# A segment mean on one core: looks 15 rows ahead, probe copies 9 rows ahead of them, and a start in two groups of three rows

## The chip, the core and the metric

The kernel runs on one core of a Trainium2 chip. TensorE (PE), VectorE (DVE), ScalarE (ACT), GpSimd (POOL) and SyncE (SP) each work through their own instructions in order and wait for each other on semaphores; 16 DMA engines move data between HBM and the on-chip memory. The metric is the device time of one execution in microseconds.

## What is computed

Ten million numbers come with sorted segment ids between 0 and 9999; the result is the mean of each segment.

```python
sums = np.zeros(num_segments); counts = np.zeros(num_segments)
np.add.at(sums, segment_ids, data)
np.add.at(counts, segment_ids, 1)
return sums / np.maximum(counts, 1)
```

## The kernel before

The numbers lie as 128 partitions of 78125, and each partition is worked off in 90 rows of 875. The ids are sorted and a segment has about a thousand numbers, so most rows hold one border between two segments, and the kernel reads only the ids around it. For a row it needs:

- probes: every 175th id of the row. One copy brings those of a whole group of rows into `pr` (`load_probes`, L161), 30 columns of 8 bytes per partition for six rows.
- the look (`first_look`, L259): six small VectorE instructions per group (`SG` L274, `ST`, `far`, `ST`, `IDX` L290, `YY` L293) that find from the probes between which two of them the border lies. `gather` (L305) then has GpSimd fetch per row and partition a window of 175 ids from there, 179 kB, into one of 18 slots of `GT`.
- the sum of that window on ScalarE (`add_ids`, L317, into `GS`); it runs up to six rows ahead of the row that ScalarE is at.
- the second look (L330) on VectorE: the border's place `KK` for a group of rows from `YY` and `GS`.
- the row itself: ScalarE sums all of it (`total`, L343), VectorE the part in front of the border (`split`, L348). Data come in tiles of two rows (875 kB) in 18 buffers, issued by SP.

Between rows VectorE also works out counts, running sums and places (steps hung up in the table `after` with `put(row, steps)`), and the last instructions make the output.

Everything is written out in one order by hand (manual schedule): the loop at L855 goes through the rows, and each engine gets its instructions in the order of that loop. Probe copies of the first `HEAD` groups are issued by SP, the others by GpSimd (L164), `X_POOL` = 18 rows ahead of their group; looks are at `X_LOOK` = 9 rows ahead. As GpSimd issues gathers and copies in order, they stand in one queue: six gathers, a copy, six gathers, a copy. A gather's slot must have been summed 18 rows earlier.

Of the kernel before, what the change touches and what calls it, by code (L numbers as in the profile page):

```python
# [17 lines left out]
P = 128  # L18
# [4 lines left out]
NR = 90  # L23
# [3 lines left out]
E = 20  # L27
NX = NR + E
FAR = float(1 << 18)
GROUPS = [6] * 15  # L30
X_PROBE = 11
X_POOL = 18
X_DATA = 26
X_LOOK = 9
RING = 18
IDS = 87
HALVES = 66
# [2 lines left out]
ND = 2 * SHIFT + 1  # L40
NT1 = 91
M1 = 8
R1 = 8 * M1 - 2
R2 = NR + 4
RM = 78
# [74 lines left out]
def kernel(  # L120
# [24 lines left out]
    def x_sum(r):  # L145
        return 6 if r < HALVES else 4
# [6 lines left out]
    snt32 = snt.bitcast(I32)  # L153
# [3 lines left out]
    bounds = [0]  # L157
# [3 lines left out]
    def load_probes(g):  # L161
        a = 0 if g == 0 else K * bounds[g] + 1
        b = min(K * bounds[g + 1] + 1, NPR)
        e = nc.sync if g < HEAD else nc.gpsimd  # L164
        e.dma_start(out=pr_flat[:, a:b], in_=ids_p[:, a * S : (b - 1) * S + 1 : S])  # L165

    tiles = {}

    def load_data(t):
        d = dpool.tile([P, 2 * L], FP32, name="data_t")  # L170
        a, b = 2 * t * L, min(2 * (t + 1) * L, D)
        c = b if t < NT - 1 else a + L
# [13 lines left out]
    def view(ap, dims):  # L186
# [3 lines left out]
        out=gt32[:, :, 0 : 2 * W : 2], in_=view(q5[:, 0, 0:1], [[0, RING], [0, W]]), func=ACT.Copy  # L190
# [30 lines left out]
        out=plast, in0=pc, scalar1=float(P - 1), scalar2=1.0e6, op0=ALU.is_equal, op1=ALU.mult  # L221
# [5 lines left out]
        out=sp_i, in0=sp_i, scalar1=3, scalar2=None, op0=ALU.arith_shift_right  # L227
    )
    nc.vector.tensor_copy(out=sp, in_=sp_i)
    ident = cpool.tile([P, P + 1], FP32, name="ident")  # L230
    nc.vector.memset(ident, 0.0)
    make_identity(nc, ident[:, 0:P])
    ones = cpool.tile([P, P], FP32, name="ones")
    nc.vector.memset(ones, 1.0)
    jj_i = cpool.tile([P, P], I32, name="jj_i")
    jj = cpool.tile([P, P], FP32, name="jj")
    nc.gpsimd.iota(jj_i, pattern=[[1, P]], base=0, channel_multiplier=0)  # L237
    nc.vector.tensor_copy(out=jj, in_=jj_i)  # L238


    VI = pr32[:, :, 0]
# [7 lines left out]
    NBP = cpool.tile([P, NX + 1], FP32, name="NBP")  # L249
    NB = NBP[:, 1:]  # L250
    QQ = cpool.tile([P, NX], FP32, name="QQ")
    FFP = cpool.tile([P, NX + 1], FP32, name="FFP")
    FF = FFP[:, 1:]
    nc.vector.memset(NBP, 0.0)
    nc.vector.memset(FFP[:, 0:1], 0.0)
    junk_v = cpool.tile([P, L], BF16, name="junk_v")
    junk_a = cpool.tile([P, L], BF16, name="junk_a")

    def first_look(g):  # L259

        a, b = bounds[g], bounds[g + 1]
        n = b - a
        far = fpool.tile([P, n], FP32, name="far", bufs=3)
        last = b == NR
        v = nc.vector

        def s1():
            if last:
                m = NR * K + 1 - NPR
                v.tensor_copy(  # L270
                    out=pr_flat.bitcast(I32)[:, 2 * NPR : 2 * (NPR + m)].rearrange("p (a b) -> p a b", b=2),
                    in_=view(snt32[:, 0:1], [[0, m], [1, 2]]),
                )
            v.tensor_reduce(out=SG[:, a:b], in_=pr32[:, a:b, 0 : 2 * K : 2], axis=AX.X, op=ALU.add)  # L274

        def s2():
            v.scalar_tensor_tensor(  # L277
                out=ST[:, a:b], in0=VI[:, a + 1 : b + 1], scalar=float(K), in1=SG[:, a:b],
                op0=ALU.mult, op1=ALU.subtract,
            )  # L280

        def s3():
            v.tensor_scalar(out=far, in0=ST[:, a:b], scalar1=0.0, scalar2=FAR, op0=ALU.is_equal, op1=ALU.mult)  # L283

        def s4():
            v.tensor_add(out=ST[:, a:b], in0=ST[:, a:b], in1=far)  # L286

        def s5():
            for c, d, w in [(a, b - 1, S), (b - 1, b, TAIL)] if last else [(a, b, S)]:
                v.scalar_tensor_tensor(  # L290
                    out=IDX[:, c:d], in0=ST[:, c:d], scalar=float(w), in1=wb[:, c:d], op0=ALU.mult, op1=ALU.add
                )
            v.scalar_tensor_tensor(  # L293
                out=YY[:, a:b], in0=ST[:, a:b], scalar=float(K + 1), in1=SG[:, a:b], op0=ALU.mult, op1=ALU.add
            )
            if last:
                v.tensor_scalar(
                    out=tl, in0=ST[:, NR - 1 : NR], scalar1=-1.0, scalar2=float(TAIL - S),
                    op0=ALU.add, op1=ALU.mult,
                )  # L300
# [57 lines left out]
    KEY = cpool.tile([P, NX + PAD], FP32, name="KEY")  # L358
    RB = cpool.tile([P, R2], FP32, name="RB")
    RX = cpool.tile([P, E], FP32, name="RX")  # L360
    PS = cpool.tile([P, R2 + 1], FP32, name="PS")
    PX = cpool.tile([P, E + 1], FP32, name="PX")
    MX = cpool.tile([P, E], FP32, name="MX")
    XX = cpool.tile([P, NX], FP32, name="XX")
    RF = cpool.tile([P, NX + PAD], FP32, name="RF")
    sel = cpool.tile([P, NT1 // 7, 7, 8], FP32, name="sel")
    tab = cpool.tile([P, NT1], FP32, name="tab")
# [10 lines left out]
    wp = cpool.tile([P, NO - C2], FP32, name="wp")  # L378
    most = cpool.tile([P, NO - C2], FP32, name="most")
    OUT = cpool.tile([P, NO], FP32, name="OUT")  # L380
    nc.vector.memset(RF, 0.0)
    nc.gpsimd.memset(tab, 0.0)
    nc.gpsimd.memset(tax, 0.0)
    nc.gpsimd.memset(shf[:, :, ND : ND + 1], 0.0)
    nc.gpsimd.memset(add, 0.0)
    nc.gpsimd.memset(xa, 0.0)
    nc.vector.memset(PS[:, 0:1], 0.0)
    nc.vector.memset(PX[:, 0:1], 0.0)
    nc.gpsimd.memset(KEY, -1000.0)
    bad = cpool.tile([P, 2 * NX + 8 + NR - RE], FP32, name="bad")  # L390
    j1 = cpool.tile([P, NX], FP32, name="j1")
    j2 = cpool.tile([P, NX], FP32, name="j2")
# [169 lines left out]
    def counts(a, b):  # L562


        n = b - a
        ps = fpool.tile([P, n], FP32, name="ps")
        ct = fpool.tile([P, n], FP32, name="ct")

        def s1():
            nc.vector.tensor_add(out=ps, in0=KK[:, a:b], in1=QQ[:, a:b])  # L570

        def s2():
            nc.vector.tensor_tensor_scan(
                out=PS[:, a + 1 : b + 1], data0=ps, data1=ps, initial=PS[:, a : a + 1],
                op0=ALU.max, op1=ALU.max,
            )
# [12 lines left out]

        return [s1, s2, s3, s4, s5]  # L590
# [183 lines left out]
            general_path(tc, fpool, ppool, data, segment_ids, out2d, jj)  # L774


    NG = len(GROUPS)
    NT = (NR + 1) // 2
    nc.vector.memset(snt32[:, 0:1], NSEG)
    nc.vector.memset(snt32[:, 1:2], 0)  # L780
    HEAD = 3


    after = defaultdict(list)
# [1 line left out]
    def put(r, steps, every=1):  # L786
        for i, f in enumerate(steps):
            after[r + i // every].append(f)

    for g in range(HEAD):  # L790
        after[-1] += first_look(g)
    after[-1] += second_look(0, GROUPS[0])
    for a, b in zip(bounds[1:], bounds[2:]):
        if b == NR:
# [6 lines left out]
            put(a + 2, second_look(a + 3, b))  # L801
    for g in range(HEAD, NG):
        if g < NG - 1:
            put(max(bounds[g] - X_LOOK, 0), first_look(g), 5)

    def mixed(p, q):
        out = []
        for i in range(max(len(p), len(q))):
            out += p[i : i + 1] + q[i : i + 1]
        return out  # L810
# [21 lines left out]
    put(64, place(0, T1, tab, [(0, C1, ND + 1, OUT[:, 0:C1]), (C1, T1, ND + 1, xa[:, 0 : T1 - C1, RM - R1])]))  # L832
    put(70, mixed(keys(72, RE)[1:], pick(nc.vector, pa[:, :, 0 : RM - R1], C1, CA - C1, R1, RM)), 2)
    put(73, check())
    look = bounds[NG - 1] - X_LOOK
    put(70, pick(nc.gpsimd, pb[:, :, 0 : RE - RM], C2, NO - C2, RM, RE), 2)
    put(look, mixed(first_look(NG - 1), counts(R1, RM)), 99)
    put(look, pick(nc.gpsimd, pb[:, :, RE - RM :], C2, NO - C2, RE, R2), 99)
    put(look + 1, mixed(edges_of(RE, NR), []), 99)
    put(look + 2, single(RE, NR, bad[:, 2 * NX + 8 :]) + verdict()[:1], 99)  # L840
# [8 lines left out]
        + spread(RS, R2, pb[:, :, RS - RM :], add[:, :, RS - RM : nb], NO - C2) + total_of(add, most), 99)  # L849
    assert max(after) <= NR - 1  # L850

    pnext = 0
    nt = 0
    gs = 0
    for r in range(-X_PROBE - X_DATA, NR):  # L855
        while pnext < NG and bounds[pnext] <= r + (X_PROBE + X_DATA if pnext < HEAD else X_POOL):
            load_probes(pnext)
            pnext += 1
            if pnext == 1:
                load_data(0)  # L860
                nt = 1
        while nt < NT and 2 * nt <= r + X_DATA:
            load_data(nt)
            nt += 1
        if r == -X_DATA:
            nc.scalar.dma_start(
                out=snt[0 : P - 1, :],
                in_=segment_ids[D : N].rearrange("(p d) -> p d", d=D)[:, 0:1],
            )
        if r == -1:  # L870
            for f in after[r][: 5 * HEAD]:
                f()
        while r >= -1 and gs < IDS and gs <= r + x_sum(gs):
            add_ids(gs)
            gs += 1
        if r == -1:
            for f in after[r][5 * HEAD :]:
                f()
        if r >= 0:
            total(r)  # L880
            split(r)
            for f in after[r]:
                f()
# [31 lines left out]
```

## Time and profile before

| | us |
|---|---|
| median of three runs | 202.51 (202.50 to 202.52) |
| the profiled execution, whole | 202.07 |
| its span, from the first instruction to the last | 200.3 |
| VectorE busy | 142.3 (71%) |
| ScalarE busy | 135.2 (67%) |
| GpSimd busy | 120.4 (60%) |
| first and last `split` (L348) start | 22.41 and 195.55 |

The busy time of GpSimd is the issuing of its copies and gathers; when they land is another matter and is read from who waits for them. TensorE has six matmuls and plays no part.

### The profile page before, as it was taken

Reading aid. Unit: us, or ns where it says so; the run is one execution under the profiler, and the core shown is the slowest. Engines: PE = TensorE matmul, PEld = TensorE weight load, DVE = VectorE, ACT = ScalarE, POOL = GpSimd, SP = SyncE. Lnnn points to the kernel's source line nnn. Section 1 sums busy time; section 2 is a strip of 40 time slices with the busy share of each in tenths; the row PEclk is TensorE's granted clock in tenths of the full one; section 3 lists DMA queues with packets and bytes.
Section 4 is the critical chain, followed back from the end, with each engine's and each line's share of the span. In section 5 each row is a group of like instructions: output and inputs, shape, how many; then the busy total and the mean of one; then the engine's idle time right before and its main releaser. Section 6 shows DMA issues by size and latency. Waiting matters only on the chain.

```text
span 200.3 us, 1426 instructions
## 1 busy us (share of the span) xinstructions
PE 1.6 (1%) x6; PEld 1.4 (1%) x6; DVE 142.3 (71%) x441; ACT 135.2 (67%) x356; POOL 120.4 (60%) x131
## 2 busy tenths in 40 slices
PE   0000000000000100000000000000000000010000
PEld 0000000000000100000000000000000000010000
DVE  6330587159628588493967989469399999999992
ACT  8011599920884949779494983949999499999700
POOL 5677778027875874747668177683746867677000
DMA  5999999999999999999999999999999995250000
GB/s 27 166 248 397 409 405 399 271 201 412 404 253 378 341 291 404 235 405 257 370 354 278 409 240 405 329 294 402 229 405 265 376 291 149 59 116 22 2 0 8
DMA packets 25363, 54.61 MB, mean 273 GB/s; under 512 B 14640, under 2 KB 15784, under 8 KB 25351
## 3 DMA queue, kind: packets, MB, share of 16 engines
q1 hardware_dynamic: 18459, 40.13, 63.4%
q0 software_dynamic: 6720, 14.38, 24.8%
q14 instruction: 12, 0.10, 0.1%
q10 hardware_dynamic: 172, 0.00, 0.1%
HBM read 56.59 MB, written 0.04 MB: 283 GB/s over the span
## 4 chain that ended last, share of the span: by engine, by line
DVE 31%; DMA 30%; issue 19%; ACT 11%; POOL 6%; POOLq 0%; ACTq 0%; DVEq 0%
DMA GT<-in_segment_ids_dram,IDX 25%; DVE junk_v L348 18%; ACT junk_a L343 7%; DMA pr<-in_segment_ids_dram 6%; ACT junk_a L317 4%; POOL GT L307 4%; DVE q L330 1%; POOL pr L165 1%; DVE far L283 1%; DVE ST L277 0%; DVE ST L286 0%; DVE IDX L290 0%; DVE shf L683 0%; DVE SG L274 0%; DVE FFP L601 0%
## 5 line engine op out<-in xcount | busy, mean ns | idle before, releaser
L307 POOL DMA_INDIRECT GT<-in_segment_ids_dram,IDX x90 | 91.3, 1015 | 61.0 <-issue 30.7
L348 DVE SCALAR_TENSOR_TENSOR junk_v<-iota,q,data_t 128x875 bf16<-128x875 f32 x90 | 100.5, 1117 | 1.4
L343 ACT ACTIVATE junk_a<-data_t 128x875 bf16<-128x875 f32 x90 | 83.6, 929 | 2.8
L317 ACT ACTIVATE junk_a<-GT 128x175 bf16<-128x175 int32 x87 | 31.3, 360 | 50.3 <-DMA GT<-in_segment_ids_dram,IDX 39.8
L330 DVE SCALAR_TENSOR_TENSOR q<-YY,GS 128x6 f32<-128x6 f32 (+1 forms) x19 | 3.6, 190 | 34.9 <-ACT junk_a L317 27.3
L165 POOL DMA_DIRECT2D pr<-in_segment_ids_dram x12 | 20.0, 1668 | 0.0
L343 ACT ACTIVATION_READ_ACCUMULATOR junk_a<-data_t 128x1 f32 x90 | 16.8, 186 | 0.0
L317 ACT ACTIVATION_READ_ACCUMULATOR junk_a<-GT 128x1 f32 x87 | 16.2, 186 | 0.0
L274 DVE TENSOR_REDUCE SG<-pr 128x6 f32<-128x30 int32 x15 | 2.7, 181 | 11.8 <-DMA pr<-in_segment_ids_dram 11.7
L348 DVE DVE_READ_ACCUMULATOR junk_v<-iota,q,data_t 128x1 f32 x90 | 7.4, 83 | 0.0
L283 DVE TENSOR_SCALAR far<-ST 128x6 f32<-128x6 f32 x15 | 3.1, 209 | 0.5
L189 ACT ACTIVATE GT<-q 128x3150 int32<-128x3150 f32 x1 | 3.0, 2992 | 0.0
L277 DVE SCALAR_TENSOR_TENSOR ST<-pr,SG 128x6 f32<-128x6 int32 x15 | 2.5, 166 | 0.5
L290 DVE SCALAR_TENSOR_TENSOR IDX<-ST,wb 128x6 int32<-128x6 f32 (+2 forms) x16 | 2.5, 161 | 0.5
L286 DVE TENSOR_TENSOR ST<-ST,far 128x6 f32<-128x6 f32 x15 | 2.5, 165 | 0.5
L293 DVE SCALAR_TENSOR_TENSOR YY<-ST,SG 128x6 f32<-128x6 f32 x15 | 2.4, 162 | 0.0
L189 ACT ACT_TABLE_LOAD x1 | 1.3, 1283 | 0.7 <-PEq L899 0.7
L715 POOL TENSOR_SCALAR pb<-pb 128x168 f32<-128x168 f32 (+1 forms) x2 | 1.6, 785 | 0.2
L555 PE MATMUL badp<-bads,ones 128*128 128x1 f32 x2 | 0.6, 362 | 108.4 <-DVE bads L554 108.4
L601 DVE TENSOR_TENSOR_SCAN FFP<-NBP,FFP,XX 128x8 f32<-128x8 f32 (+3 forms) x5 | 1.3, 265 | 0.1
L238 DVE CAST jj<-jj_i 128x128 f32<-128x128 int32 x1 | 0.8, 839 | 0.7 <-POOL jj_i L237 0.7
L668 DVE TENSOR_TENSOR sel<-sel,RF 128x280 f32<-128x280 f32 (+1 forms) x3 | 1.2, 410 | 0.1
(129 smaller groups left out, 47.4 us busy)
## 6 DMA issues: line engine op xcount, KB each, us to landing
data_t<-in_data_dram SPq DMA_DIRECT2D x44, 875.0 KB
GT<-in_segment_ids_dram,IDX POOLq DMA_INDIRECT x90
data_t<-in_data_dram SPq DMA_DIRECT2D x1, 437.5 KB
pr<-in_segment_ids_dram POOLq DMA_DIRECT2D x11, 30.0 KB
data_t<-in_data_dram SPq DMA_DIRECT2D x1, 125.0 KB
pr<-in_segment_ids_dram SPq DMA_DIRECT2D x2, 30.0 KB
out_dram<-OUT SPq DMA_DIRECT2D x1, 36.6 KB
pr<-in_segment_ids_dram SPq DMA_DIRECT2D x1, 31.0 KB
```

What stands on the lines that cost most here:

```text
L165: e.dma_start(out=pr_flat[:, a:b], in_=ids_p[:, a * S : (b - 1) * S + 1 : S])
L189: nc.scalar.activation(out=gt32[:, :, 0 : 2 * W : 2], in_=view(q5[:, 0, 0:1], [[0, RING], [0, W]]), func=ACT.Copy)
L274: v.tensor_reduce(out=SG[:, a:b], in_=pr32[:, a:b, 0 : 2 * K : 2], axis=AX.X, op=ALU.add)
L277: v.scalar_tensor_tensor(out=ST[:, a:b], in0=VI[:, a + 1 : b + 1], scalar=float(K), in1=SG[:, a:b], op0=ALU.mult, op1=ALU.subtract,)
L283: v.tensor_scalar(out=far, in0=ST[:, a:b], scalar1=0.0, scalar2=FAR, op0=ALU.is_equal, op1=ALU.mult)
L286: v.tensor_add(out=ST[:, a:b], in0=ST[:, a:b], in1=far)
L290: v.scalar_tensor_tensor(out=IDX[:, c:d], in0=ST[:, c:d], scalar=float(w), in1=wb[:, c:d], op0=ALU.mult, op1=ALU.add)
L307: nc.gpsimd.indirect_dma_start(out=GT[:, r % RING, :], out_offset=None, in_=ids2d[:], in_offset=bass.IndirectOffsetOnAxis(ap=IDX[:, r : r ...
L317: nc.scalar.activation(out=junk_a[:, 0:W], in_=gt32[:, r % RING, 0 : 2 * W : 2], func=ACT.Copy, accum_out=GS[:, r : r + 1],)
L330: nc.vector.scalar_tensor_tensor(out=KK[:, a:b], in0=YY[:, a:b], scalar=float(S // K), in1=GS[:, a:b], op0=ALU.mult, op1=ALU.subtract,)
L343: nc.scalar.activation(out=junk_a[:, 0:n], in_=d, func=ACT.Copy, accum_out=t)
L348: nc.vector.scalar_tensor_tensor(out=junk_v[:, 0:n], in0=iota[:, 0:n], scalar=KK[:, r : r + 1], in1=d, op0=ALU.is_lt, op1=ALU.mult, accum_ ...
```

## The change

- Groups: the first six rows become two groups of three, so there are 16 groups; the first four (18 rows) have their looks ahead of row 0 (`HEAD` = 4, before 3).
- Looks are 15 rows ahead instead of 9, all six instructions in one row also for the last group, whose look was at row 75 and is now at row 69.
- Probe copies stand 24 rows ahead of their group. GpSimd issues the first one (16 columns) as its first instruction, SP the next four, between the first data tiles; the sixth is issued by GpSimd between the gathers of the start.
- VectorE's constants that the first look doesn't need move behind that look, GpSimd's fills (`blanks`) behind row 0.

```diff
-GROUPS = [6] * 15
-X_PROBE = 11
-X_POOL = 18
+GROUPS = [3, 3] + [6] * 14
+HEAD = 4
-X_LOOK = 9
+X_LOOK = 15
+X_PROBE = X_LOOK + 9
...
-        e = nc.sync if g < HEAD else nc.gpsimd
+        e = nc.sync if 0 < g <= HEAD else nc.gpsimd
...
+    load_probes(0)
...
-    nc.vector.memset(ident, 0.0)
-    make_identity(nc, ident[:, 0:P])
...
+    def constants():
+
+        nc.vector.tensor_copy(out=jj, in_=jj_i)
+        nc.vector.memset(ident, 0.0)
+        make_identity(nc, ident[:, 0:P])
...
+    def blanks():
+
+        nc.gpsimd.memset(tab, 0.0)
...
-        after[-1] += first_look(g)
+        after[-1] += first_look(g) + ([constants] if g == 0 else [])
...
-            put(max(bounds[g] - X_LOOK, 0), first_look(g), 5)
+            put(bounds[g] - X_LOOK, first_look(g), 5)
...
-    look = bounds[NG - 1] - X_LOOK
+    put(bounds[NG - 1] - X_LOOK, first_look(NG - 1), 5)
+    put(0, [blanks])
+    look = 75
...
-    put(look, mixed(first_look(NG - 1), counts(R1, RM)), 99)
+    put(look, counts(R1, RM), 99)
...
+        if r == -X_DATA:
+            load_probes(1)
+            load_data(0)
+            load_probes(2)
+            load_probes(3)
+            load_data(1)
+            load_probes(4)
+            nt = 2
+        if r >= 0:
+            for g in range(HEAD + 2, NG):
+                if bounds[g] == r + X_PROBE:
+                    load_probes(g)
...
+            for i, f in enumerate(after[r][:looks]):
                 f()
+                if i == 2 * 5:
+                    load_probes(HEAD + 1)
```

GpSimd's instructions from the last fills of the start on, before (`GT` are gathers, `pr` probe copies; the second row stands for rows 0 to 17, the fourth for rows 18 to 23):

```order
L389 MEMSET KEY 128x112
L307 DMA GT<-in_segment_ids_dram,IDX 128x175 x18
L165 DMA pr<-in_segment_ids_dram 128x30x1 x2
L307 DMA GT<-in_segment_ids_dram,IDX 128x175 x6
L165 DMA pr<-in_segment_ids_dram 128x30x1
```

The same with the change, from GpSimd's last iota on (the gathers of rows 0 to 2, 3 to 5, 6 to 17, 18 to 23 and 24 to 29):

```order
L236 IOTA jj_i 128x128
L303 DMA GT<-in_segment_ids_dram,IDX 128x175 x3
masks.py:197 MEMSET ident 128x128
masks.py:199 AFFINE_SELECT ident<-ident 128x128
L303 DMA GT<-in_segment_ids_dram,IDX 128x175 x3
L165 DMA pr<-in_segment_ids_dram 128x30x1
L303 DMA GT<-in_segment_ids_dram,IDX 128x175 x12
L392 MEMSET tab 128x91
...
L397 MEMSET KEY 128x112
L303 DMA GT<-in_segment_ids_dram,IDX 128x175 x6
L165 DMA pr<-in_segment_ids_dram 128x30x1
L303 DMA GT<-in_segment_ids_dram,IDX 128x175 x6
```

One copy instead of two stands ahead of row 18's gather, and the fills have moved from ahead of the first gather to behind the eighteenth. In both, the copy behind the gathers of rows 18 to 23 is the one for rows 30 to 35.

VectorE from row 0 on, before (L330 is a second look, L348 a row, L274 the first instruction of a look, here the one for rows 18 to 23, at row 9):

```order
L330 SCALAR_TENSOR_TENSOR q_74<-YY,GS 128x6
L348 SCALAR_TENSOR_TENSOR junk_v,q_74<-iota,q_74,data_t 128x875 x6
...
L348 SCALAR_TENSOR_TENSOR junk_v,q_74<-iota,q_74,data_t 128x875 x4
L274 TENSOR_REDUCE SG<-pr 128x6
L277 SCALAR_TENSOR_TENSOR ST<-pr,SG 128x6
```

The same with the change (the look for rows 18 to 23 is at row 3):

```order
L326 SCALAR_TENSOR_TENSOR q_75<-YY,GS 128x3
L344 SCALAR_TENSOR_TENSOR junk_v,q_75<-iota,q_75,data_t 128x875 x3
...
L344 SCALAR_TENSOR_TENSOR junk_v,q_75<-iota,q_75,data_t 128x875
L270 TENSOR_REDUCE SG<-pr 128x6
L273 SCALAR_TENSOR_TENSOR ST<-pr,SG 128x6
```

The look has moved up by six rows of L348, and its probe copy with it: SP issues it at the start. From row 15 on, the look at a row is the one that stood six rows later before, and its copy is one that GpSimd issues one group of gathers later than the copy of the look that stood there.

## Rows read from the trace of the kernel before

**Rows 1.** The page, busy time of each engine (share of the span), instructions.

```profile
PE 1.6 (1%) x6; PEld 1.4 (1%) x6; DVE 142.3 (71%) x441; ACT 135.2 (67%) x356; POOL 120.4 (60%) x131
```

**Rows 2.** The page, DMA queues (q1: SP, q0: GpSimd): packets, MB, share.

```profile
q1 hardware_dynamic: 18459, 40.13, 63.4%
q0 software_dynamic: 6720, 14.38, 24.8%
```

**Rows 3.** Waits of all engines: in total us, times, longest us.

```profile
ACT junk_a L317 <- DMA GT<-in_segment_ids_dram,IDX: 39.8, 16, 9.0
...
DVE q L330 <- ACT junk_a L317: 27.3, 9, 5.1
...
DVE SG L274 <- DMA pr<-in_segment_ids_dram: 11.7, 3, 6.2
```

**Rows 4.** Busy time by stretch: PE, PEld, DVE, ACT, POOL, clock, DMA share, GB/s.

```profile
120.00:145.00 25.00, 0.00 (x0) 0.00 (x0) 16.98 (x46) 18.25 (x49) 16.72 (x16) 1.00 1.04 331
145.00:170.00 25.00, 0.00 (x0) 0.00 (x0) 24.46 (x77) 20.78 (x57) 16.87 (x16) 1.00 0.96 301
```

**Rows 5.** VectorE's timeline, 128 to 172 us: start, duration, instruction, [idle before].

```profile
143.38 0.19 DVE L330 SCALAR_TENSOR_TENSOR q<-YY,GS 128x6 f32<-128x6 f32 x1 [3.41 <-ACT junk_a L317]
...
149.45 0.18 DVE L274 TENSOR_REDUCE SG<-pr 128x6 f32<-128x30 int32 x1
...
159.82 0.18 DVE L274 TENSOR_REDUCE SG<-pr 128x6 f32<-128x30 int32 x1
...
161.22 1.12 DVE L348 SCALAR_TENSOR_TENSOR junk_v<-iota,q,data_t 128x875 bf16<-128x875 f32 x1
```

**Rows 6.** ScalarE's timeline, window sums of rows 18, 24 and 72.

```profile
50.39 0.36 ACT L317 ACTIVATE junk_a<-GT 128x175 bf16<-128x175 int32 x1 [9.01 <-DMA GT<-in_segment_ids_dram,IDX]
...
62.66 0.36 ACT L317 ACTIVATE junk_a<-GT 128x175 bf16<-128x175 int32 x1 [3.08 <-DMA GT<-in_segment_ids_dram,IDX]
...
158.56 0.36 ACT L317 ACTIVATE junk_a<-GT 128x175 bf16<-128x175 int32 x1 [2.68 <-DMA GT<-in_segment_ids_dram,IDX]
```

**Rows 7.** GpSimd's timeline: copies, the gathers of rows 18, 24 and 84.

```profile
31.07 3.35 POOL L165 DMA_DIRECT2D pr<-in_segment_ids_dram  x2
43.93 1.09 POOL L307 DMA_INDIRECT GT<-in_segment_ids_dram,IDX  x1 [9.51 <-issue]
...
51.55 1.67 POOL L165 DMA_DIRECT2D pr<-in_segment_ids_dram  x1
53.53 1.04 POOL L307 DMA_INDIRECT GT<-in_segment_ids_dram,IDX  x1 [0.31 <-ACT junk_a L343]
...
172.74 1.11 POOL L307 DMA_INDIRECT GT<-in_segment_ids_dram,IDX  x1 [1.40 <-DVE IDX L290]
```

**Rows 8.** DMA rate, 170 to 182 us, 40 slices of 0.3 us.

```profile
GB/s 61 121 238 107 0 0 0 0 0 0 0 0 0 0 27 154 201 121 14 84 168 201 70 61 131 93 47 164 140 187 168 42 93 177 247 28 15 89 19 0
```

**Rows 9.** DMA rate, 50 to 90 us, 40 slices of 1 us.

```profile
GB/s 394 417 416 375 415 399 410 196 135 139 304 380 407 385 413 393 403 413 338 186 128 167 312 417 370 412 394 423 403 407 332 151 128 181 398 381 406 408 398 413
```

**Rows 10.** ScalarE's timeline, window sum of row 3.

```profile
19.07 0.36 ACT L317 ACTIVATE junk_a<-GT 128x175 bf16<-128x175 int32 x1 [3.70 <-DMA GT<-in_segment_ids_dram,IDX]
```

**Rows 11.** All engines' timeline, the start.

```profile
3.71 0.15 DVE L229 CAST sp<-sp_i 128x1 f32<-128x1 int32 x1
...
4.78 0.17 POOL L382 MEMSET tab<- 128x91 f32 x1
...
5.72 0.18 DVE L274 TENSOR_REDUCE SG<-pr 128x6 f32<-128x30 int32 x1
...
7.72 1.20 POOL L307 DMA_INDIRECT GT<-in_segment_ids_dram,IDX  x1 [1.38 <-DVE YY L293]
...
8.41 30.61 SPq L173 DMA_DIRECT2D data_t<-in_data_dram  x16
```

**Rows 12.** DMA rate, 130 to 170 us, 40 slices of 1 us.

```profile
GB/s 134 164 342 409 381 389 395 400 430 370 345 142 129 164 360 401 399 401 431 420 382 406 267 144 167 247 372 431 382 403 375 383 379 274 82 113 240 127 149 158
```

More of the change, by code (lines that the diff above doesn't have):

```diff
@@ L230 @@
     ident = cpool.tile([P, P + 1], FP32, name="ident")
-    nc.vector.memset(ident, 0.0)
-    make_identity(nc, ident[:, 0:P])
     ones = cpool.tile([P, P], FP32, name="ones")
-    nc.vector.memset(ones, 1.0)
     jj_i = cpool.tile([P, P], I32, name="jj_i")
@@ L237 @@
     nc.gpsimd.iota(jj_i, pattern=[[1, P]], base=0, channel_multiplier=0)
-    nc.vector.tensor_copy(out=jj, in_=jj_i)
     VI = pr32[:, :, 0]
@@ L253 @@
     FF = FFP[:, 1:]
-    nc.vector.memset(NBP, 0.0)
-    nc.vector.memset(FFP[:, 0:1], 0.0)
     junk_v = cpool.tile([P, L], BF16, name="junk_v")
@@ L380 @@
     OUT = cpool.tile([P, NO], FP32, name="OUT")
[L381 to L389, printed above, removed]
+    def constants():
+        nc.vector.tensor_copy(out=jj, in_=jj_i)
+        nc.vector.memset(ident, 0.0)
+        make_identity(nc, ident[:, 0:P])
+        nc.vector.memset(ones, 1.0)
+        nc.vector.memset(RF, 0.0)
+        nc.vector.memset(PS[:, 0:1], 0.0)
+        nc.vector.memset(PX[:, 0:1], 0.0)
+        nc.vector.memset(NBP, 0.0)
+        nc.vector.memset(FFP[:, 0:1], 0.0)
+    def blanks():
+        nc.gpsimd.memset(tab, 0.0)
+        nc.gpsimd.memset(tax, 0.0)
+        nc.gpsimd.memset(shf[:, :, ND : ND + 1], 0.0)
+        nc.gpsimd.memset(add, 0.0)
+        nc.gpsimd.memset(xa, 0.0)
+        nc.gpsimd.memset(KEY, -1000.0)
     bad = cpool.tile([P, 2 * NX + 8 + NR - RE], FP32, name="bad")
@@ L774, in finish @@
             general_path(tc, fpool, ppool, data, segment_ids, out2d, jj)
+    nc.vector.memset(snt32[:, 0:1], NSEG)
+    nc.vector.memset(snt32[:, 1:2], 0)
     NG = len(GROUPS)
     NT = (NR + 1) // 2
-    nc.vector.memset(snt32[:, 0:1], NSEG)
-    nc.vector.memset(snt32[:, 1:2], 0)
-    HEAD = 3
     after = defaultdict(list)
@@ L790 @@
     for g in range(HEAD):
-        after[-1] += first_look(g)
+        after[-1] += first_look(g) + ([constants] if g == 0 else [])
+    looks = len(after[-1])
     after[-1] += second_look(0, GROUPS[0])
@@ L850 @@
     assert max(after) <= NR - 1
-    pnext = 0
     nt = 0
     gs = 0
[L855 to L861, printed above, removed]
+    for r in range(-X_DATA, NR):
+        if r == -X_DATA:
[10 more added lines that the diff above has]
+                    load_probes(g)
         while nt < NT and 2 * nt <= r + X_DATA:
@@ L870 @@
         if r == -1:
-            for f in after[r][: 5 * HEAD]:
+            for i, f in enumerate(after[r][:looks]):
                 f()
+                if i == 2 * 5:
+                    load_probes(HEAD + 1)
         while r >= -1 and gs < IDS and gs <= r + x_sum(gs):
@@ L876 @@
         if r == -1:
-            for f in after[r][5 * HEAD :]:
+            for f in after[r][looks:]:
                 f()
```

## The prediction

> **What bounds the kernel now.** I read the page first. No engine is busy throughout: VectorE leads with 142.3 us, 71% of the span [rows 1], so something makes it wait. The queue lines come next: SP's data copies and GpSimd's id copies together take 88% of the 16 DMA engines' span [rows 2], which leaves the memory side little room. Then the waits over all engines, where the reader is to see one chain: ScalarE waited 39.8 us in 16 pieces for gathers (the window of ids per row, tile `GT`), and VectorE waited 27.3 us in nine pieces for ScalarE's sums of those windows; three looks out of 15 waited for a probe copy, so the other twelve found theirs landed [rows 3]. VectorE never waited for data. The table by stretches puts the waits in their place: from 120 to 145 us VectorE is busy 16.98 of 25, from 145 to 170 it is busy 24.46 of 25, with the DMA share at 1.04 and 0.96 [rows 4]. So there are two stages: until row 60 the gathers set the pace (the last such wait ends at 143.38 [rows 5]); behind it VectorE works without a gap to the end.
>
> What sets the pace of the gathers? ScalarE's wait for the first window of a group ends at 50.39, 62.66 and so on to 158.56, nine groups of six rows later [rows 6]: (158.56 - 50.39) / 9 = 12.02 us per group. GpSimd is not the bound, it had issued early: the gather of row 24 at 53.53, 9.1 us before its ids were added, while the gather of row 18 at 43.93, issued after 9.5 us of idle time with nothing ahead of it, needed 6.5 us [rows 6, 7]. Near the end, with no data moving, the gather issued at 172.74 shows as a burst that ends near 175.5, under 3 us [rows 7, 8]. So beside the data copies the transfers that GpSimd issues stand in line. What they take there: in the rate by 1 us slices a probe copy shows as a dip from 400 to some 130 GB/s, 3.5 to 4 us long (57 to 61, 68 to 72, 80 to 84) [rows 9]; I take 3.7. Then a gather takes (12.02 - 3.7) / 6 = 1.39 us. The dips also show the order: the copy issued at 51.55 moves from 57 on, behind the six gathers issued before it [rows 7, 9].
>
> The Trainium skill, "DMA: Bandwidth & Descriptors", section "Anatomy of one DMA", fits such a transfer at 2.0 us plus its bytes at 436 GB/s, an estimate of 2.4 us for a gather's 179 kB. By that rule no line builds up, and the time would be rival A's. The lone gather at the end agrees with it; the 9.1 us beside data do not, and the measurement decides.
>
> **The change, part by part.**
>
> *Order in the line.* Before, GpSimd sends 18 gathers, two copies (31.07), nothing until 43.93, six gathers, a copy. The gather of row 3 lands at 19.07 [rows 10]. The copy for rows 30 to 35, issued at 51.55, is through at about 61.2 [rows 7, 9]. After, the line behind row 3 is: 2 gathers, one copy, 12 gathers, 6 gathers, and the copy for rows 30 to 35: 20 x 1.39 + 2 x 3.7 = 35.2, so 54.2. The idle stretch and one copy (now SP's) are gone: the line runs 7.0 us earlier, if row 3 lands when it did. From there on it was saturated before and stays so: 12.02 a group.
>
> *The start.* It shifts that 7.0. For: VectorE reaches its first look at 5.72 only because 1.9 us of other constants stand behind the cast at 3.71 [rows 11]; they now come behind the look. Against: GpSimd first issues a copy of 16 columns (30 columns took 1.67 [rows 7], so 1.0 to 1.7), and its iotas, which VectorE's casts wait for, move back by that; about 0.5 us is left. Row 3's window came after a wait of 3.70 us [rows 10], when SP's stream of tiles, issued from 8.41 [rows 11], had set in; SP now sends another copy before its third tile, which puts the stream off by up to 3 us. Bounds for row 5 and the copy behind it: 2.5 us earlier (all of that counts) to 1 us later (GpSimd's first copy lands after VectorE is ready). I take 1.1 earlier, nearer to the middle than to either end. The line is then 8.1 us ahead.
>
> *Looks 15 rows ahead.* This is the term that takes the gain away. VectorE works in order, and a look needs its probe copy. The look at row 63 was for rows 72 to 77; now it is for rows 78 to 83, whose copy stands one group (12.02 us) further back in the line. That copy's dip ends at about 156.5 [rows 12]; minus 8.1 is 148.4. Before, the look at row 63 ran at 149.45 [rows 5], so it starts 1.0 earlier. Without its wait of 3.41 us at row 60 [rows 5] VectorE would be there by about 146, so it stands idle for 2.4. All looks from row 15 on wait like that: queued behind each are VectorE's next rows, whose windows landed before. The look at row 69 needs the last copy, of 26 instead of 30 columns: 12.02 - 0.5 = 11.5 behind the one before, 148.4 + 11.5 = 159.9. VectorE's own work from row 63's look to row 69's, 159.82 - 149.45 = 10.4, would have it there at 158.8, so the copy decides. Before: 159.82. So at row 69 the changed kernel is level, +0.1.
>
> *After row 69* there is one look less: row 75's has moved up. A look took 1.4 at row 69 (159.82 to 161.22 [rows 5]); row 75's ran in the gaps of other work, so between 0.5 and 1.4, I take 1.0. VectorE's remaining work is otherwise the same, and it is the bound there [rows 4].
>
> *Costed at nothing.* VectorE's constants, 1.9 us, stand in its wait for the first windows. GpSimd's fills, which ran from 4.78 on and were over before the gather at 7.72 [rows 11], now stand between the gathers of rows 17 and 18, under 2 us, covered by some 8 us of line; without that they would delay row 18 by themselves. Splitting the first group starts row 0 earlier, but row 15's look waits in any case. SP's extra copy delays its tiles by some 3 us; no wait for data stands among VectorE's waits, so that has cover.
>
> Sum: +0.1 - 1.0 = -0.9 us. The profiled execution took 202.07 us with a span of 200.3; the median of the three runs is 202.51, and against that the forecast is 201.6 us. With the start between its bounds it runs from 200.2 to 203.7.
>
> **Rivals.**
>
> *A: the looks find their copies.* If the line is not served in order or is faster than 1.39 and 3.7 once more is queued, the early looks cost nothing; row 60 moves by the full 8.1 and VectorE saves a look: 202.5 - 9.1 = 193.4; half of it, with 0.6 us less per group, gives about 196. For it: twelve looks did not wait [rows 3]. Against: windows issued six deep still came 12.02 a group. The Trainium skill, same page, section "Queues, rings and completion order", says that a DMA engine takes turns between queues packet by packet. By that rule the line's share beside data does not grow when gathers are issued earlier, which speaks against A and against the change. Chance 0.17.
>
> *B: slower, by the first copy.* Everything in the line hangs on GpSimd's first copy. If it lands near 8 us instead of 5.2 (beside data the copy issued at 51.55 needed 9.7 us [rows 7, 9]), the line is 2.7 us later, 5.4 ahead instead of 8.1, and the look at row 69 starts at 162.6: 201.6 + 2.7 = 204.3. It turns to a loss once the line is less than 7.2 us ahead. Against it: at the start no data stream runs. Chance 0.21.
>
> *C: no change that shows.* What the start gains is small, the looks only trade a wait for gathers for a wait for copies, and the line is 7 to 7.6 us ahead: 202.5. Chance 0.19.
>
> **How the numbers follow.** The forecast has 0.43. A measurement of this kernel can tell 0.2%, 0.4 us, from no change. Faster than 202.1: two thirds of the forecast's own range and all of A, a little of C: 0.47. Slower than 202.9: B, and small parts of the forecast and C: 0.31. The rest, 0.22, is within. The range for 8 in 10 goes from 196.0 (A's half, leaving out A's full gain) to 204.6 (B's price); the forecast's own range, 200.2 to 203.7, lies inside it.
>
> **What would show it.** Right: VectorE's largest wait is the look (`SG`) for probe copies, some ten times 2 to 5 us, and its wait for ScalarE's window sums is nearly gone; windows still come 12 us a group; the look at row 69 starts near 160. The gather of row 18 follows the fills without an idle stretch. Wrong: looks without waits and VectorE full from row 50 on (A); a first gather issued after 9 us (B); groups under 11.5 us apart would break the figure of the line itself.

## The result: slower by 3 us, and the profile after

The changed kernel takes 205.62 us (median, 205.08 to 206.11), the kernel before 202.51: a ratio of 1.015, 95% interval 1.0119 to 1.018. The forecast was 201.6 us and its range ended at 204.6, so the sign and the range were both wrong. The profiled execution took 205.08 us with a span of 203.3; before it was 202.07 and 200.3. Runs more than 1.5% above the fastest of their kernel count in no ratio; below, that concerns two of the four runs with halved data copies on the kernel before.

The page, engine line and SP's and GpSimd's queues, changed kernel:

```profile
PE 1.6 (1%) x6; PEld 1.4 (1%) x6; DVE 142.2 (70%) x448; ACT 135.3 (67%) x356; POOL 120.1 (59%) x131
...
q1 hardware_dynamic: 20267, 40.15, 64.3%
q0 software_dynamic: 6688, 14.36, 22.9%
```

No engine works more than before [rows 1] and the bytes are the same [rows 2]. SP now issues more of the copies in 8-byte pieces, which shows as 1800 more packets. So the loss is in waits. The waits, changed kernel (us in total, times, longest):

```profile
ACT junk_a L313 <- DMA GT<-in_segment_ids_dram,IDX: 45.6, 18, 10.8
DVE SG L270 <- DMA pr<-in_segment_ids_dram: 31.6, 12, 4.5
DVE q L326 <- ACT junk_a L313: 17.9, 4, 9.1
```

Against [rows 3]: looks wait for their probe copies 12 times instead of three, 31.6 us instead of 11.7, and VectorE's wait for window sums has shrunk from 27.3 to 17.9. That is the exchange of one wait for another which was forecast. But it happens later than forecast. VectorE's looks at rows 15, 63 and 69, changed kernel (start, duration, instruction, [idle before]):

```profile
57.50 0.18 DVE L270 TENSOR_REDUCE SG<-pr 128x6 f32<-128x30 int32 x1 [4.52 <-DMA pr<-in_segment_ids_dram]
...
153.08 0.18 DVE L270 TENSOR_REDUCE SG<-pr 128x6 f32<-128x30 int32 x1 [2.49 <-DMA pr<-in_segment_ids_dram]
...
164.47 0.18 DVE L270 TENSOR_REDUCE SG<-pr 128x6 f32<-128x30 int32 x1 [0.84 <-DMA pr<-in_segment_ids_dram]
```

The forecast had 148.4 and 159.9 for the last two. Both are 4.6 to 4.7 us late, and the first is already 4.4 late (57.50 against 54.2 - 1.1 = 53.1). So the time was lost ahead of row 15 and then carried to the end. ScalarE's window sums of rows 18 and 72, changed kernel, show the pace between:

```profile
49.19 0.36 ACT L313 ACTIVATE junk_a<-GT 128x175 bf16<-128x175 int32 x1
...
154.56 0.36 ACT L313 ACTIVATE junk_a<-GT 128x175 bf16<-128x175 int32 x1 [3.58 <-DMA GT<-in_segment_ids_dram,IDX]
```

(154.56 - 49.19) / 9 = 11.7 us per group, where [rows 6] gave 12.02. The pace is much the same; the start is not. All engines at the start, changed kernel:

```profile
0.74 0.47 SPq L165 DMA_DIRECT2D pr<-in_segment_ids_dram  x1
1.30 1.41 POOL L165 DMA_DIRECT2D pr<-in_segment_ids_dram  x1 [0.85 <-POOLq L917]
2.81 0.24 POOL L197 IOTA wb_i<- 128x89 int32 x1
3.17 1.01 DVE L199 CAST wb<-wb_i 128x90 f32<-128x90 int32 x1 [1.72 <-POOL wb_i L198]
8.59 0.17 DVE L270 TENSOR_REDUCE SG<-pr 128x3 f32<-128x15 int32 x1 [2.62 <-DMA pr<-in_segment_ids_dram]
10.45 1.09 POOL L303 DMA_INDIRECT GT<-in_segment_ids_dram,IDX  x1 [5.71 <-DVE SG L270]
...
21.09 0.36 ACT L313 ACTIVATE junk_a<-GT 128x175 bf16<-128x175 int32 x1 [1.82 <-DMA GT<-in_segment_ids_dram,IDX]
...
24.67 0.36 ACT L313 ACTIVATE junk_a<-GT 128x175 bf16<-128x175 int32 x1 [1.00 <-DMA GT<-in_segment_ids_dram,IDX]
30.71 0.36 ACT L313 ACTIVATE junk_a<-GT 128x175 bf16<-128x175 int32 x1 [5.58 <-DMA GT<-in_segment_ids_dram,IDX]
```

GpSimd's first copy, issued at 1.30, was there at about 8.5, 7.2 us later. It costs twice: GpSimd's iotas wait behind its issue, so VectorE's cast waits 1.72 us, and then the look stands another 2.62 us. The first look is at 8.59 instead of 5.72 and the first gather at 10.45 instead of 7.72 [rows 11]. The last three rows are the window sums of rows 3, 5 and 6: row 3's is at 21.09 (19.07 before [rows 10]), and between rows 5 and 6 the copy in GpSimd's queue shows as 5.58 us of waiting.

### The profile page after: what moved, and what is told of

Same layout as the page of the kernel before. It is cut to its first block, busy times and chain, and to the rows that moved or that the text cites. A ratio compares the mean times of both kernels' runs of the same rounds, so it can differ in the third digit from the quotient of the medians.

```text
span 203.3 us, 1435 instructions
## 1 busy us (share of the span) xinstructions
PE 1.6 (1%) x6; PEld 1.4 (1%) x6; DVE 142.2 (70%) x448; ACT 135.3 (67%) x356; POOL 120.1 (59%) x131
## 4 chain that ended last, share of the span: by engine, by line
DMA 65%; DVE 18%; issue 9%; POOL 5%; ACT 1%; POOLq 0%; DVEq 0%; ACTq 0%
DMA GT<-in_segment_ids_dram,IDX 47%; DMA pr<-in_segment_ids_dram 17%; DVE junk_v L344 9%; POOL GT L303 4%; ACT junk_a L313 1%; ACT junk_a L339 1%; DVE far L279 0%; DVE SG L270 0%; DVE IDX L286 0%; DVE q L326 0%; DVE add L760 0%; DVE ST L282 0%; DVE ST L273 0%; DVE FFP L610 0%; DVE most L768 0%
## 5 line engine op out<-in xcount | busy, mean ns | idle before, releaser
L270 DVE TENSOR_REDUCE SG<-pr 128x6 f32<-128x30 int32 (+1 forms) x16 | 2.9, 181 | 31.6 <-DMA pr<-in_segment_ids_dram 31.6
L326 DVE SCALAR_TENSOR_TENSOR q<-YY,GS 128x3 f32<-128x3 f32 (+1 forms) x20 | 3.2, 159 | 18.0 <-ACT junk_a L313 17.9
L760 POOL TENSOR_TENSOR xa<-pa,RG 128x528 f32<-128x528 f32 x1 | 1.2, 1247 | 5.9 <-DVE RG L757 5.9
L279 DVE TENSOR_SCALAR far<-ST 128x6 f32<-128x6 f32 (+1 forms) x16 | 2.8, 175 | 0.5
L286 DVE SCALAR_TENSOR_TENSOR IDX<-ST,wb 128x6 int32<-128x6 f32 (+3 forms) x17 | 2.7, 165 | 0.5
L273 DVE SCALAR_TENSOR_TENSOR ST<-pr,SG 128x6 f32<-128x6 int32 (+1 forms) x16 | 2.7, 168 | 0.6
L282 DVE TENSOR_TENSOR ST<-ST,far 128x6 f32<-128x6 f32 (+1 forms) x16 | 2.7, 167 | 0.5
L289 DVE SCALAR_TENSOR_TENSOR YY<-ST,SG 128x6 f32<-128x6 f32 (+1 forms) x16 | 2.6, 161 | 0.0
L199 DVE CAST wb<-wb_i 128x90 f32<-128x90 int32 x1 | 1.0, 1015 | 1.7 <-POOL wb_i L198 1.7
```

The lines of the kernel that those rows point to most:

```text
L273: v.scalar_tensor_tensor(out=ST[:, a:b], in0=VI[:, a + 1 : b + 1], scalar=float(K), in1=SG[:, a:b], op0=ALU.mult, op1=ALU.subtract,)
L286: v.scalar_tensor_tensor(out=IDX[:, c:d], in0=ST[:, c:d], scalar=float(w), in1=wb[:, c:d], op0=ALU.mult, op1=ALU.add)
L326: nc.vector.scalar_tensor_tensor(out=KK[:, a:b], in0=YY[:, a:b], scalar=float(S // K), in1=GS[:, a:b], op0=ALU.mult, op1=ALU.subtract,)
```

## The experiments

Two theories stood after this. T: two separate failings, a first copy that comes late and looks that are held by their copies. The rivals: either one alone, or the groups of three rows. L, on the pace itself: it comes from sharing the DMA engines with the data.

**The first copy by SP again.**

```diff
-        e = nc.sync if 0 < g <= HEAD else nc.gpsimd
+        e = nc.sync if g <= HEAD else nc.gpsimd
```

> The changed kernel with its first copy (16 columns) issued by SP instead of GpSimd; looks stay 15 rows ahead. Theory T (both parts count: the late first gather, 10.45 us instead of 7.72, delays the whole line of GpSimd's transfers, and looks 15 ahead wait for a copy one group further back in it): first gather near 7.7, the line 2.7 us earlier, the look at row 69 at about 161.8 instead of 164.5, time 202.9; VectorE's looks still wait some 30 us for copies. Rival R1 (only the start costs): the same 202.9. Rival R2 (only the lead costs, a late start is absorbed): 205.6, unchanged.

198.93 us (198.72 to 199.64), 0.9855 of the kernel before (0.9809 to 0.9901). One instruction moved back gives 6.7 us, two and a half times the 2.7 that T expected. The start of that run:

```profile
3.80 0.17 DVE L270 TENSOR_REDUCE SG<-pr 128x3 f32<-128x15 int32 x1
...
5.71 1.25 POOL L303 DMA_INDIRECT GT<-in_segment_ids_dram,IDX  x1 [2.96 <-DVE SG L270]
...
14.81 0.36 ACT L313 ACTIVATE junk_a<-GT 128x175 bf16<-128x175 int32 x1 [0.44 <-DMA GT<-in_segment_ids_dram,IDX]
```

The look is 4.8 us earlier than in the changed kernel (8.59), the first gather 4.7 and row 3's window 6.3. T had put the first gather at 7.7; it came 2.0 us before that. The look at 3.80 does not wait at all; it shows that moving the constants behind it was worth the 1.9 us that the prediction saw in [rows 11]. The waits for copies are still there, which fits the second half of T but does not show yet that they cost anything:

```profile
DVE SG L270 <- DMA pr<-in_segment_ids_dram: 36.9, 13, 5.3
```

**The first copy by GpSimd, in the kernel before.** The opposite edit, with no other part of the change:

```diff
-        e = nc.sync if g < HEAD else nc.gpsimd
+        e = nc.sync if 0 < g < 3 else nc.gpsimd
...
+    load_probes(0)
...
-            load_probes(pnext)
+            if pnext > 0:
+                load_probes(pnext)
```

> The kernel before with one edit: its first probe copy (30 columns) is issued by GpSimd as its first instruction instead of by SP. Theory S (the first copy by GpSimd lands some 7 us after its issue, and everything hangs on it): the first look starts at 9 to 10 us instead of 5.72, the first gather at 11 to 12 us instead of 7.72, and the kernel takes 205 to 208 us. Rival (the late start of the changed kernel is due to its groups of three rows and the copy between its gathers of rows 5 and 6, the first copy is hidden): within 0.5 us of the kernel before.

206.37 us (206.16 to 206.64) against 202.07, ratio 1.0208 (1.0157 to 1.026): 4.3 us lost. Its start:

```profile
1.29 1.97 POOL L165 DMA_DIRECT2D pr<-in_segment_ids_dram  x1 [0.85 <-POOLq L902]
...
10.24 0.18 DVE L276 TENSOR_REDUCE SG<-pr 128x6 f32<-128x30 int32 x1 [1.88 <-DMA pr<-in_segment_ids_dram]
...
12.12 1.09 POOL L309 DMA_INDIRECT GT<-in_segment_ids_dram,IDX  x1 [3.14 <-DVE ST L288]
```

The first gather is 4.4 us later than at 7.72, and the kernel 4.3 us slower: with groups of six rows too, a late start comes out at the end in full. The groups of three are not needed for that loss.

**Why that copy is slow.** The changed kernel, with SP's first instruction held until VectorE has done its casts, so that GpSimd's copy moves alone (SP's first tile then also goes ahead of its first copy):

```diff
+    hold = dpool.tile([P, 2 * L], FP32, name="data_t")
+    nc.vector.memset(hold[:, 0:1], 0.0)
...
-        d = dpool.tile([P, 2 * L], FP32, name="data_t")
+        d = hold if t == 0 else dpool.tile([P, 2 * L], FP32, name="data_t")
...
-            load_probes(1)
             load_data(0)
+            load_probes(1)
```

> The changed kernel, its first copy by GpSimd as there, but with nothing of SP's beside it: SP's copies and data tiles wait until VectorE has done its casts (a one-column fill of the first data tile that stands behind them), so SP starts near 6 us instead of 0.74. In the changed kernel the first copy was issued at 1.30 and its look, which waited 2.62 us for it, ran at 8.59. Theory P (the copy is slow by the way GpSimd issues it): the look for rows 0 to 2 still starts at 8 us or later. Theory C (it is slow because SP's copies of 8-byte pieces and first tiles move beside it): the look starts at 6 to 6.5 us, right behind VectorE's casts, without a wait. The time by itself says little, as SP's stream starts later: 202 to 208 us.

The start, the copy's landing (KB, us from issue) and the DMA rate from 0 to 20 us in 40 slices of 0.5 us:

```profile
1.30 1.41 POOL L165 DMA_DIRECT2D pr<-in_segment_ids_dram  x1 [0.85 <-POOLq L919]
...
5.89 0.17 DVE L272 TENSOR_REDUCE SG<-pr 128x3 f32<-128x15 int32 x1
...
5.98 0.42 SPq L175 DMA_DIRECT2D data_t<-in_data_dram  x1
...
pr<-in_segment_ids_dram POOLq DMA_DIRECT2D x1, 16.0 KB, 4.0
...
GB/s 0 0 0 0 0 0 2 20 10 0 0 0 0 0 169 266 392 420 434 122 92 190 137 219 54 27 195 63 68 31 19 169 97 106 320 423 426 392 350 150
```

The same row of the changed kernel, with the busy share of the 16 DMA engines in tenths above it:

```profile
DMA  0001899499999999694999495899999999999799
GB/s 0 0 0 2 12 14 144 112 336 378 406 365 92 13 20 6 8 14 7 14 16 17 5 127 98 266 392 378 392 384 93 100 192 98 237 145 380 305 375 367
```

Alone, the copy is a small burst between 3.0 and 4.5 us: (2 + 20 + 10) x 0.5 us is its 16 kB. It has landed 4.0 us after its issue, and the look at 5.89 does not wait for it. In the changed kernel SP's first probe copy moves from 2 to 3 us at 12 to 14 GB/s and keeps the DMA engines 80 to 90% busy with that, SP's first tile of data follows up to 6.5, then come SP's next copies, and GpSimd's copy needs 7.2 us. So theory C: company makes it slow. Whether SP's 8-byte pieces or its tile do more of it is not separated. The run took 202.17 us (201.28 to 202.39), 1.0024 of the kernel before (0.9997 to 1.005): some 3 us less than the changed kernel, although SP's whole stream starts 5.2 us later (5.98 against 0.74). What stays with theory P is the issue itself, behind which the iotas still wait: the look is at 5.89, not at 3.80.

**Looks 9 rows ahead**, as before (copies with them, 18 ahead), with the first copy by GpSimd and by SP, and 11 ahead by SP:

```diff
-X_LOOK = 15
+X_LOOK = 9
```

> The changed kernel with looks 9 rows ahead as before (copies 18), everything else of the change kept, GpSimd's first copy too. T: looks find their copies, waits of SG under 5 us in all; but the look for rows 18 to 23 is at row 9 again, near 44, so the idle stretch of GpSimd comes back and the line is about where it was before: 203.0. R1 (only the start): 205.6. R2 (only the lead): 199 to 202, since the line is then 3 us ahead of before.

> The changed kernel with both taken back: first copy by SP, looks 9 ahead; left are the two groups of three, the constants set later and SP's fourth copy. T: the look at row 9 some 2 us earlier than with GpSimd's copy, gather of row 18 near 42 instead of 43.9: 200.5. R1: 202.9. R2: 202.

> The changed kernel with the first copy by SP and looks 11 rows ahead (copies 9 rows ahead of them, 20 of their group). Theory T: at 9 rows the looks found nearly all their copies (196.82 us), at 15 they waited 36.9 us (198.93 us); at 11 a copy stands as far back in the queue as at 9 or one group further for part of the looks, so waits for it between those two and a time of 196.5 to 198.5 us. Rival G (GpSimd's queue ran dry for the 0.3 to 2.7 us between groups at 9 rows, and earlier looks fill that): 195 to 196.4 us.

203.74, 196.82 and 194.63 us (ratios 1.0101, 0.9739 and 0.9616; intervals 1.0054 to 1.0148, 0.9698 to 0.9781, 0.9563 to 0.967). Looks 9 rows ahead are 1.9 and 2.1 us faster than 15, so their waits did cost something. The second time lies below all three expectations (200.5, 202.9 and 202): the first copy by SP is worth 6.9 us here too (203.74 to 196.82), where T had put 2.5. But at 9 rows GpSimd runs dry again, as before the change [rows 7]. The gather of row 18 with the first copy by GpSimd, whose look runs at 43.99:

```profile
45.75 1.00 POOL L303 DMA_INDIRECT GT<-in_segment_ids_dram,IDX  x1 [7.74 <-ACT junk_a L313]
```

At 11 rows both are small: looks wait 9.7 us in all, and the gather of row 18 comes after 3.6 us of idle time, where it was 5.6 at 9 rows with the same first copy. That was the rival's direction (the queue is kept filled); the time lies below T's range and a little below the rival's.

**Looks 15 rows ahead, their copies further ahead**, by SP and by GpSimd:

```diff
-X_PROBE = X_LOOK + 9
+X_PROBE = X_LOOK + 15
```

> The changed kernel with the first copy by SP and looks 15 rows ahead, as in the run that gave 198.93 us, but with each probe copy 30 rows ahead of its group instead of 24, so one group of gathers earlier in GpSimd's queue. Theory T (the looks are held by the place of their copy in the queue): VectorE's waits of SG for pr, 36.9 us in 13 pieces there, fall under 10 us, the windows set the pace alone as with looks 9 rows ahead, 196.82 us there; 196 to 198 us. Rival R (looking 15 rows ahead costs by itself, through VectorE's order or the 18 slots, and the copies were only where the wait showed): 198.5 to 199.5 us, with the waits turned up elsewhere.

> The changed kernel with one edit: probe copies 30 rows ahead of their group instead of 24; the first copy stays with GpSimd. With the first copy by SP this edit was worth 6.2 us (198.93 to 192.75). Theory T (two separate failings, the late first copy and the looks held by their copies, that add up): looks wait under 10 us behind the start, 199 to 200.5 us, faster than the kernel before. Rival (with the late start the windows are late anyway and take the place of the copies): 203 to 205.5 us.

192.75 us (0.9534, 0.9485 to 0.9583) and 200.08 us (0.9906, 0.9877 to 0.9935). The first is the fastest of all and beats both kernels; T had expected 196 to 198. The waits of the looks and of the second looks in it:

```profile
DVE q L326 <- ACT junk_a L313: 23.4, 9, 3.9
...
DVE SG L270 <- DMA pr<-in_segment_ids_dram: 6.9, 2, 5.1
```

The wait of the looks has gone from 36.9 us to 6.9, all of it at the start, and windows set the pace again. The gain doesn't come from earlier windows. The look at row 69 and the window sum of row 72, with copies 24 ahead and then 30 ahead (first copy by SP in both):

```profile
157.82 0.18 DVE L270 TENSOR_REDUCE SG<-pr 128x6 f32<-128x30 int32 x1 [0.94 <-DMA pr<-in_segment_ids_dram]
...
147.84 0.36 ACT L313 ACTIVATE junk_a<-GT 128x175 bf16<-128x175 int32 x1 [3.25 <-DMA GT<-in_segment_ids_dram,IDX]
```

```profile
152.55 0.18 DVE L270 TENSOR_REDUCE SG<-pr 128x6 f32<-128x30 int32 x1
...
150.83 0.36 ACT L313 ACTIVATE junk_a<-GT 128x175 bf16<-128x175 int32 x1 [2.27 <-DMA GT<-in_segment_ids_dram,IDX]
```

Row 72's window is 3.0 us later with copies 30 ahead, and yet VectorE reaches row 69's look 5.3 us earlier: what the late copies held up was VectorE, in front of rows whose windows were there. The second run keeps the late first copy and lands where T said the sum of two failings would:

| | copies 24 ahead | copies 30 ahead | gain |
|---|---|---|---|
| first copy by GpSimd | 205.62 | 200.08 | 5.5 |
| first copy by SP | 198.93 | 192.75 | 6.2 |
| gain | 6.7 | 7.3 | |

**Without data beside the gathers** (tiles from row 36 on reuse the first 18, so the sums of rows 36 to 89 use other rows' data):

```diff
     def load_data(t):
+        if t >= 18:
+            tiles[t] = tiles[t - 18]
+            return
```

> The changed kernel without the data copies behind the first 18 tiles of two rows: later rows reuse those tiles, so data of rows 36 to 89 are left out of the sums. Theory L (the pace of 12 us a group of six gathers and one copy is set by sharing the DMA engines with the data): from row 36 on ScalarE's waits for windows vanish, windows of two groups follow each other at VectorE's or ScalarE's own pace, 8.5 to 10 us, and the kernel takes 180 to 192 us. Rival (GpSimd's issuing or the 18 slots set the pace, whatever moves beside): groups stay 11.5 to 12.1 us apart up to row 60, 203 to 206 us.

185.88 us in one run. Busy time in one stretch, changed kernel and this one (DVE, ACT, POOL busy after PE and PEld, then clock, DMA share, GB/s):

```profile
100.00:125.00 25.00, 0.00 (x0) 0.00 (x0) 20.53 (x65) 19.21 (x53) 16.96 (x16) 1.00 1.05 320
```

```profile
100.00:125.00 25.00, 0.00 (x0) 0.00 (x0) 24.20 (x69) 23.96 (x67) 20.12 (x19) 1.00 0.53 98
```

The window sums of rows 36 and 72 start at:

```profile
80.12 0.36 ACT L316 ACTIVATE junk_a<-GT 128x175 bf16<-128x175 int32 x1
...
137.65 0.36 ACT L316 ACTIVATE junk_a<-GT 128x175 bf16<-128x175 int32 x1
```

9.6 us a group instead of 11.7, without a wait in front: theory L, by one run. VectorE (24.20 of 25 us) is near its limit now, and so is GpSimd: it issues six gathers and a copy in some 9.6 us, with no pause over 0.31 us between two of them. So 9.6 is what issuing takes, and the transfers need no more than that; how much less is not shown. That it is the DMA engines which data and gathers share, and not something behind them, is argued from the DMA share (1.05 and 0.53).

**Data in halves**, one copy per row instead of per two, on the kernel before and on the fastest version:

```diff
-        nc.sync.dma_start(out=d[:, 0 : c - a], in_=data_p[:, a:c])
+        for h in range(a, c, L):
+            nc.sync.dma_start(out=d[:, h - a : h - a + L], in_=data_p[:, h : h + L])
```

> The kernel before with each data tile loaded by two DMAs of 875 columns (3500 bytes per partition) instead of one of 1750 (7000 bytes). If the line's pace beside data is set by turns between the queues, packet by packet (theory L), shorter data packets give the line more turns: a gather under 1.3 us in the line instead of 1.39, groups of windows some 9.5 to 10.5 us apart instead of 12.0, VectorE full from about row 45 on, 188 to 195 us. If the pace is a share of the bytes, or the latency of look, issue and landing (rival): groups 12 us apart, 202 to 203 us.

> The version that gave 192.75 us (first copy by SP, looks 15 rows and copies 30 rows ahead), with each data tile loaded by two copies of 875 columns, one per row, instead of one of 1750. On the kernel before this edit alone gave 196.49 us instead of 202.21, with groups some 11.5 instead of 12.0 us apart. Theory L (what moves beside the gathers sets their pace, and shorter data packets leave them more of the engines): groups under 11.8 us apart, 187 to 190.5 us. Rival (the earlier order has used up what the edit gave): 192 to 193.5 us.

On the kernel before: four runs from 193.29 to 197.03 us against 202.21; the ratio is 0.9639 (0.9543 to 0.9736), so some 5 to 9 us gained. The time is at the upper end of what L expected, the pace is not. Window sums of rows 18 and 72:

```profile
49.42 0.36 ACT L318 ACTIVATE junk_a<-GT 128x175 bf16<-128x175 int32 x1 [8.12 <-DMA GT<-in_segment_ids_dram,IDX]
...
153.91 0.36 ACT L318 ACTIVATE junk_a<-GT 128x175 bf16<-128x175 int32 x1 [3.44 <-DMA GT<-in_segment_ids_dram,IDX]
```

(153.91 - 49.42) / 9 = 11.6 us a group, where L had 9.5 to 10.5 and the rival 12.0. On the fastest version: 195.15 us (194.9 to 195.43), 2.4 us slower than with whole tiles, against both expectations. Rows now wait for data there, which they did once in the version with whole tiles:

```profile
DVE junk_v L345 <- DMA data_t<-in_data_dram: 25.3, 26, 2.4
...
ACT junk_a L340 <- DMA data_t<-in_data_dram: 21.2, 22, 3.0
```

ScalarE's wait for windows has shrunk there from 38.5 us to 12.0. So shorter copies shift the engines' time from data to gathers. That helps where data are ahead, and harms where the gathers have caught up.

**All probe copies by SP**, on the fastest version:

```diff
-        e = nc.sync if g <= HEAD else nc.gpsimd
+        e = nc.sync
```

> The version that gave 192.75 us, with all probe copies issued by SP between its data copies, none by GpSimd. Theory Q (a copy holds up the gathers because it stands in GpSimd's queue, 3.7 us a group): groups come 8.5 to 10 us apart, VectorE becomes the bound, 180 to 188 us. Rival W (a copy's 8-byte pieces take the DMA engines' time from everything, in whichever queue it stands): groups stay 11 to 12 us apart, 191 to 197 us, or more if a copy behind waiting data copies comes late for its look.

201.39 us (0.9967, 0.9951 to 0.9982), 8.6 slower than the fastest version. A copy in SP's queue stands behind data copies that wait for a free buffer (SP waited 45.2 us in nine pieces for ScalarE's row sums). One look, and the waits of all:

```profile
54.81 0.18 DVE L270 TENSOR_REDUCE SG<-pr 128x6 f32<-128x30 int32 x1 [21.13 <-DMA pr<-in_segment_ids_dram]
```

```profile
DVE SG L270 <- DMA pr<-in_segment_ids_dram: 43.3, 12, 21.1
```

It doesn't decide whether a copy's price of 3.7 us belongs to the queue or to the engines, since the late copies cover it.

## Why the prediction was wrong

**The step that failed is "The start."** Its term was -1.1 us, bounded by -2.5 and +1. Row 5's window was added at 24.67; in the trace before it was

```profile
21.73 0.36 ACT L317 ACTIVATE junk_a<-GT 128x175 bf16<-128x175 int32 x1 [1.07 <-DMA GT<-in_segment_ids_dram,IDX]
```

That is 2.9 us later, outside the bounds. Row 3's window was 2.0 later than [rows 10] instead of 1.1 earlier, 3.1 us of miss. The line from there to the copy for rows 30 to 35 took 57.50 - 21.09 = 36.4 us instead of 35.2, another 1.2. Together 4.3 of the 4.4 us by which row 15's look was late.

Within that step two sentences were wrong. "1.0 to 1.7" for the issue was about right (1.41), but the iotas started 2.0 us later (2.81), as GpSimd also waited 0.85 first instead of 0.40; all of what the constants gave back was spent, where "about 0.5 us" was to be left. And the landing was put at 5.2 us, with "at the start no data stream runs" against a later one. The run with the copy alone shows that to be good for an idle chip (issued at 1.30, landed 4.0 us later) and wrong for this one: SP's probe copies and its first tile move there. The trace before had the evidence. The three waits for copies in [rows 3] were read only as "the other twelve found theirs landed"; two of them stand at the start, the third at row 9:

```profile
3.86 4.51 SPq L165 DMA_DIRECT2D pr<-in_segment_ids_dram  x2
...
11.15 0.18 DVE L274 TENSOR_REDUCE SG<-pr 128x6 f32<-128x30 int32 x1 [4.30 <-DMA pr<-in_segment_ids_dram]
...
13.45 0.18 DVE L274 TENSOR_REDUCE SG<-pr 128x6 f32<-128x30 int32 x1 [1.24 <-DMA pr<-in_segment_ids_dram]
...
42.16 0.18 DVE L274 TENSOR_REDUCE SG<-pr 128x6 f32<-128x30 int32 x1 [6.18 <-DMA pr<-in_segment_ids_dram]
```

Copies that SP issued from 3.86 us on held the second look until 11.15. That was the nearest row for a probe copy at the start, some 7 us, and it would have made the start some +3 and the forecast near 205.7. The third is the look for rows 18 to 23: the idle time of GpSimd ahead of row 18's gather [rows 7], which the prediction counted as a gain of the new order, was for the most part a look held by its copy already.

**Rival B was the case that came**, with its sign (a first gather after 9 us) and its mechanism; its price of 2.7 us was short by 1.3: at row 3 it was 0.4 short (3.1), the line up to row 15 added 1.2 and the way to row 69 another 0.3, and the end gave 0.6 back. Why the line took 1.2 us more is open.

**The wait that takes the place of the one removed was right.** Looks waited twelve times, up to 4.5 us; the four waits for window sums that are left end with the one at 48.13; groups stayed 11.7 apart. The gather of row 18 came without an idle stretch, at 37.89 instead of 43.93, and gave nothing at the end:

```profile
37.89 1.01 POOL L303 DMA_INDIRECT GT<-in_segment_ids_dram,IDX  x1 [0.17 <-issue]
```

That the copies hold the looks was argued then and is shown now: with copies one group of gathers earlier in GpSimd's queue and nothing else changed, the kernel takes 6.2 us less (5.5 with the late first copy).

**The end was nearly right.** From row 69's look to the end of the span it took 203.3 - 164.47 = 38.8 us, before 200.3 - 159.82 = 40.5: -1.6 where -1.0 was forecast. The sum then closes: +4.6 at row 69, -0.6 here, 4.0 us above the forecast, as measured (205.62 - 201.6).

**The rule on turns between queues** (the Trainium skill, "DMA: Bandwidth & Descriptors", section "Queues, rings and completion order": a DMA engine serves its queues in turn, packet by packet) was weighed against rival A. The run without data agrees with it in kind, 9.6 instead of 11.7 us a group. The runs with halved copies agree in direction only: some 5 to 9 us gained on one kernel, 2.4 lost on another, where data became late.

## What to carry to other kernels

The first transfer of a chain whose links run in order is worth its delay in full or more: in the kernel before 4.4 us at the first gather were 4.3 us at the end, in the changed kernel 4.7 were 6.7. Bound it by the nearest row that has the same company, not by a quiet one. And when a step is moved ahead, move what feeds it by as much, counted in places of its own queue. Here the copies were moved by six rows as the looks were, but in GpSimd's queue they stayed behind the same gathers: looks six rows earlier lost 2 us with copies 9 rows in front of them, and gained 4 us (196.82 to 192.75) with copies 15 rows in front.

## What the runs showed of the hardware

- A copy of 16 kB in 8-byte pieces by GpSimd landed 4.0 us after its issue when nothing else moved, and was waited for until 7.2 us after it beside SP's copies of the same kind and SP's first tile. One of 30 columns took 8.9 us (1.29 to about 10.2) in the kernel before with its first copy by GpSimd.
- A copy in 8-byte pieces by SP kept the 16 DMA engines 80 to 90% busy while it moved 12 to 14 GB/s.
- GpSimd's first DMA, with 1.41 us of issue, put the instructions behind it 2.0 us later (iotas at 2.81 instead of 0.85).
- Without data beside them, six gathers and a copy pass in no more than 9.6 us, which is what GpSimd needs to issue them (busy 20.12 of 25 us); beside the data they need 11.7 us at a DMA share of 1.05.
- Data copies of half the length moved time from the data to the gathers (waits for windows 38.5 to 12.0 us, VectorE's waits for data 3.6 to 25.3); in the two kernels tried it gained where the gathers were late and lost where data became late.
